# A two-block network on one core: the ends of five stages put in program order

## The chip, the core and the metric

The kernel runs on one core of a Trainium2 chip. The metric is the device time of one execution, in microseconds (us). TensorE (PE) multiplies, ScalarE (ACT) and VectorE (DVE) do elementwise work, GpSimd (POOL) takes some of it over, and SyncE (SP) issues the DMAs. Each engine runs its own instructions in the order in which the program was built, and waits on semaphores for the others.

## What is computed

The input `x` has 256 rows of 1024 columns, and six stages each add something to it:

```python
x = x + pool_mixer(rmsnorm(x))                                  # trailing means, a linear map per group
x = x + conv_ffn(rmsnorm(x))                                    # (silu(conv3(h Wg)) * (h Wv)) Wout, width 2816
x = x + chunk_attention(rmsnorm(x))                             # 16 heads, softmax, o @ w_o
x = x + conv_ffn(rmsnorm(x))
x = x + (sigmoid(ga) * y_a + sigmoid(gb) * y_b) @ w_out         # retention and stick-breaking branches
x = x + peer(rmsnorm(x))                                        # 8 heads, top-16 of 128 x 128 keys, experts u, v
```

All of it is float32.

## The kernel before

The 256 rows lie in two blocks of 128 (b = 0, 1), the 1024 columns in two halves of 512 (h = 0, 1). A float32 product is made of three matmuls on parts in a shorter type (`mm3`, lines 111 to 113): high part by high part, high by low, low by high. So every weight slab that a DMA brings (`raw`) is split: ACT writes the high part `whi` (line 73), DVE the low part `wlo` (line 81), in pieces of 512 columns; `to_pool` is the number of slabs whose low parts POOL makes instead. `prefetch(n)` sees to it that n slabs are split.

**The turn of a stage** is what stands between two stages. The stage's last products end in four accumulators `acc[b][h]`. For each, `add_to_x` (DVE, line 255) adds the accumulator to `x`, and `half_done` makes what the next stage multiplies: four transposes of 128 x 128 on PE (line 230, in `transposed`), four high parts `hT` times the norm's gain on ACT (line 236), four low parts on DVE (line 238). The squares for the norm (`sq`, line 164) are ACT's too. There are four such turns: from the first ffn to attention, from attention to the second ffn, from the second ffn to the branches, and from the branches to peer. A fifth place of the kind lies inside the branches, where the gated mix is transposed (`mT`) ahead of the last product of that stage.

**The last products before a turn.** The ffn has 22 tiles f of its inner width. `up_mm(f)` computes tile f before the gate, `act(f)` applies convolution, silu and gate on DVE and ACT and ends in the two parts `gTh` (line 216) and `gTl` (line 217), and `down(f)` multiplies them with the output weights. The products of f = 19, 20 and 21 are left for the end and written for one (b, h) after the other. In `out_proj`, which ends attention and the branches, they are those of k = 4 to 7; k is a pair of heads in attention, and the last pair is k = 7: its softmax weights `s` are scaled by DVE (line 679), transposed by PE (`pt_ps`, line 687), copied by ACT (`pT`, line 688), multiplied with the values (`o_ps`, line 722) and split into `oTh` and `oTl`.

**What sets the order.** Outside blocks marked `manual_schedule` a planner orders each engine's instructions: an instruction that is written later may go ahead of one that would wait. Inside such a block the engines named keep the order in which the program is written. The ends of the stages lie outside such blocks; `up_mm(0)` of the second ffn lies inside one for PE alone, and peer's products inside one for three engines.

Of the kernel before, what the change touches and what calls it, by code (L numbers as in the profile page):

```python
# [8 lines left out]
F32 = mybir.dt.float32  # L9
# [11 lines left out]
KT = D // 128  # L21
# [26 lines left out]
class K:  # L48
# [13 lines left out]
    def split_slab(self, later=False):  # L62
        nc = self.nc
        raw = self.loaded.pop(0)
        cols, n = raw.shape[1], self.piece
        low = nc.vector.tensor_tensor
        if self.to_pool:
            self.to_pool -= 1
            low = nc.gpsimd.tensor_tensor
        hi = self.wp.tile([128, cols], F32R, tag="hi", name="whi", bufs=self.nsplit)  # L70
        lo = self.wp.tile([128, cols], F32R, tag="lo", name="wlo", bufs=self.nsplit)
        for c in range(0, cols, n):
            i = nc.scalar.activation(hi[:, c:c + n], raw[:, c:c + n], AF.Copy)  # L73
            if self.pin:
                self.tc.keep_in_program_order(i)
                self.pin = False
# [13 lines left out]
    def start_stream(self, srcs):  # L90
# [3 lines left out]
        self.to_pool = 0  # L94
        self.pin = False

# [61 lines left out]
    def rms(self, b, out=None):  # L158
# [99 lines left out]
    def proj(self, hT, halves=2, by_block=False):  # L258
# [11 lines left out]
        if by_block:  # L270
            self.prefetch(3)
            ws = [self.next() for _ in range(halves)]
            for b in range(2):
                for half in range(halves):
                    for k in range(4):
                        part(half, k, b)
            return ps
# [25 lines left out]
    def pool_mixer(self):  # L303
        nc = self.nc
        st = self.stage
        W = WINDOWS[-1]
        order = self.tc.manual_schedule(engines={nc.tensor.engine, nc.vector.engine, nc.scalar.engine})

# [188 lines left out]
    def ffn(self, l):  # L497
# [8 lines left out]
        def up_mm(f):  # L506
# [5 lines left out]
            for k0 in range(0, KT, n):  # L512
                for i in range(2):
                    for k in range(k0, k0 + n):
                        c = slice(i * 1024 + k * 128, i * 1024 + (k + 1) * 128)
# [28 lines left out]
        if l == 0:  # L544

            with self.tc.manual_schedule(engines={nc.tensor.engine, nc.vector.engine, nc.scalar.engine}):
                up_mm(0)
# [22 lines left out]
        for f in range(2, FT, 2):  # L570
# [9 lines left out]
            if f < FT - 2:  # L580
                down(f)
        for b in range(2):
# [141 lines left out]
    def out_proj(self, rows):  # L724
# [7 lines left out]
        ws = [self.next() for _ in range(2)]  # L732
        for b in range(2):
            for h in range(2):
                for i in range(2):
                    for j in range(2):
                        self.down_part(acc, rows(4 + 2 * i + j), 4 + 2 * i + j, *ws[i], j, KT, (b,), (h,))
                self.add_to_x(acc[b][h], b, h * 512)
                self.half_done(b, h)


    def branches(self):
# [4 lines left out]
        ret = self.retention(hT, r)  # L747
        mixes = []
        for h in range(2):
            m = st.tile([128, 2, 512], F32, tag="rv", name="mix", bufs=2)  # L750
            mixes.append(m)
            for i, src in enumerate((ret, sb)):
# [9 lines left out]
        mT = []  # L762
        for h in range(2):
# [176 lines left out]
    def peer(self, rt, wq_scope):  # L940
# [3 lines left out]
        def side(gen, upto):  # L944
# [10 lines left out]
            return True  # L955

        order = ExitStack()
        order.enter_context(tc.manual_schedule(engines={nc.tensor.engine, nc.vector.engine, nc.scalar.engine}))
        with ExitStack() as ctx:
# [8 lines left out]
            prev, xn = None, []  # L968
            self.to_pool = 7
            for h in range(8):  # L970
# [14 lines left out]
                for k0 in range(0, KT, n):  # L985
                    for m in range(2):
                        for k in range(k0, k0 + n):
                            c = slice(m * 1024 + k * 128, m * 1024 + (k + 1) * 128)
# [469 lines left out]
```

## Time and profile before

| what | us |
|---|---|
| median of 3 runs | 1555.27 (1555.16 to 1555.55) |
| the profiled execution | 1555.51 |
| its span in the trace | 1553.8 |

PE is busy for 1545.5 us of the span, DVE for 1142.0, ACT for 835.3, POOL for 78.0. The span is what the trace covers; 1.7 us of the execution's time lie outside it. The chain of work that ended last runs over PE for 97% of the span.

### The profile page before, as it was taken

The numbers are of one execution on the slowest core, as the hardware profiler recorded it, in microseconds if no ns is written. First come the engines' busy times: TensorE is split into PE (matmuls) and PEld (weight loads), VectorE is DVE, ScalarE is ACT, GpSimd is POOL, SyncE is SP. The second block draws the span as 40 slices with busy tenths as digits, with TensorE's granted clock in tenths as the row PEclk, the third lists the DMA queues.
The fourth block names the chain that finished last, engine by engine and source line by source line (L and its number), as shares of the span: only waits on it lengthen the run. The fifth ranks groups of instructions, "written<-read, shape, count | busy, mean of one in ns | idle before, by whom it ended". The sixth has DMA issues, their size and how long they took to land.

```text
span 1553.8 us, 26327 instructions
## 1 busy us (share of the span) xinstructions
PE 1545.5 (99%) x10142; PEld 1383.9 (89%) x10142; DVE 1142.0 (73%) x2497; ACT 835.3 (54%) x1544; POOL 78.0 (5%) x93
## 2 busy tenths in 40 slices
PE   9999999999999999999999999999999999999999
PEld 9999987789999887888999999999999888888887
DVE  6777688876776887685689988888898655555554
ACT  7555576565555656444554555544444544454443
POOL 0000030020000202000450000000000000000000
PEclk9999999999999999999999999999999999999999
DMA  5645564335555643545426555555555656666664
GB/s 217 236 172 208 191 231 148 136 136 190 192 191 187 202 170 109 193 154 178 173 84 202 185 182 164 165 166 172 164 163 175 191 192 193 196 193 192 197 193 149
DMA packets 58157, 277.11 MB, mean 178 GB/s; under 512 B 6448, under 2 KB 7344, under 8 KB 41520
## 3 DMA queue, kind: packets, MB, share of 16 engines
q1 hardware_dynamic: 58032, 275.44, 53.5%
q8 instruction: 79, 1.29, 0.3%
q14 instruction: 46, 0.38, 0.1%
HBM read 274.36 MB, written 1.05 MB: 177 GB/s over the span
## 4 chain that ended last, share of the span: by engine, by line
PE 97%; DVE 2%; ACT 1%; DMA 0%; issue 0%; SPq 0%; POOL 0%; ACTq 0%; DVEq 0%; POOLq 0%
PE acc L112 16%; PE acc L113 16%; PE acc L111 16%; PE hps L111 8%; PE hps L112 8%; PE hps L113 8%; PE up L112 5%; PE up L113 5%; PE up L111 5%; PE gps L1066 2%; PE qps L112 1%; PE qps L111 1%; PE qps L113 1%; PE pt L230 1%; PE o_ps L722 1%; PE scps L1173 0%
## 5 line engine op out<-in xcount | busy, mean ns | idle before, releaser
L73 ACT ACTIVATE whi<-raw 128x512 fp32r<-128x512 f32 (+1 forms) x752 | 549.1, 770 | 356.7 <-PE acc L113 150.0
L81 DVE TENSOR_TENSOR wlo<-raw,whi 128x512 fp32r<-128x512 f32 (+1 forms) x568 | 447.7, 814 | 129.2 <-ACT whi L73 129.1
L111 PE MATMUL hps<-hn,whi 128*128 128x256 f32 x1024 | 291.9, 285 | 0.0
L112 PE MATMUL hps<-hn,whi 128*128 128x256 f32 x1024 | 285.8, 279 | 0.0
L113 PE MATMUL hps<-hn,wlo 128*128 128x256 f32 x1024 | 285.6, 279 | 0.0
L112 PE MATMUL up<-hT,whi 128*128 128x256 f32 x704 | 196.4, 279 | 0.8 <-DVE hT L238 0.8
L111 PE MATMUL up<-hT,whi 128*128 128x256 f32 x704 | 197.2, 280 | 0.0
L113 PE MATMUL up<-hT,wlo 128*128 128x256 f32 x704 | 196.4, 279 | 0.0
L112 PE MATMUL acc<-wlo,hn 128*128 128x512 f32 x504 | 196.1, 389 | 0.0
L113 PE MATMUL acc<-whi,hn 128*128 128x512 f32 x504 | 196.1, 389 | 0.0
L111 PE MATMUL acc<-whi,hn 128*128 128x512 f32 x504 | 196.1, 389 | 0.0
L112 PEld LDWEIGHTS hps<-hn,whi 128*128 128x128 f32 x1024 | 192.7, 188 | 0.0
L111 PEld LDWEIGHTS hps<-hn,whi 128*128 128x128 f32 x1024 | 192.6, 188 | 0.0
L113 PEld LDWEIGHTS hps<-hn,wlo 128*128 128x128 f32 x1024 | 192.4, 188 | 0.0
L88 DVE TENSOR_TENSOR wlo<-raw,whi 128x1024 fp32r<-128x1024 f32 (+1 forms) x132 | 158.7, 1203 | 14.6 <-ACT whi L73 13.7
L112 PEld LDWEIGHTS up<-hT,whi 128*128 128x128 f32 x704 | 132.4, 188 | 2.4 <-DVE hT L238 1.0
L111 PEld LDWEIGHTS up<-hT,whi 128*128 128x128 f32 x704 | 132.3, 188 | 1.5
L113 PEld LDWEIGHTS up<-hT,wlo 128*128 128x128 f32 x704 | 132.3, 188 | 0.2
L112 PE MATMUL acc<-wlo,hT 128*128 128x512 f32 x304 | 120.1, 395 | 0.0
L113 PE MATMUL acc<-whi,hT 128*128 128x512 f32 x304 | 119.8, 394 | 0.0
L111 PE MATMUL acc<-whi,hT 128*128 128x512 f32 x304 | 119.2, 393 | 0.0
L112 PEld LDWEIGHTS acc<-wlo,hn 128*128 128x128 f32 x504 | 94.6, 188 | 19.7
(290 smaller groups left out, 2395.1 us busy)
## 6 DMA issues: line engine op xcount, KB each, us to landing
raw<-in_peer_u SPq DMA_DIRECT2D x128, 512.0 KB, 3.6
raw<-in_peer_v SPq DMA_DIRECT2D x128, 512.0 KB, 3.6
raw<-in_wup SPq DMA_DIRECT2D x44, 1024.0 KB, 5.0
raw<-in_win SPq DMA_DIRECT2D x26, 1024.0 KB, 4.9
raw<-in_wdn SPq DMA_DIRECT2D x22, 1024.0 KB, 5.0
raw<-in_wqkv SPq DMA_DIRECT2D x12, 1024.0 KB, 4.9
raw<-in_wo SPq DMA_DIRECT2D x8, 1024.0 KB, 4.8
raw<-in_peer_wq SPq DMA_DIRECT2D x8, 1024.0 KB, 4.9
```

Of the source, the lines that this page charges most:

```text
L73: i = nc.scalar.activation(hi[:, c:c + n], raw[:, c:c + n], AF.Copy)
L81: low(*args, op=OP.subtract)
L88: self.nc.vector.tensor_tensor(*self.low_parts.pop(0), op=OP.subtract)
L111: mm(ps, lh, rh, start=start, stop=False, skip_group_check=True)
L112: mm(ps, lh, rl, start=False, stop=False, skip_group_check=True)
L113: mm(ps, ll, rh, start=False, stop=stop, skip_group_check=True)
L230: nc.tensor.transpose(pt[:, j, :], src[:, (k + j) * 128:(k + j + 1) * 128], self.ident)
L722: mm(o[hs, t], v[b][:, hs], w[e][:, c], start=b == 0, stop=b == 1, skip_group_check=True)
L1066: nc.tensor.matmul(ps[:, j], jh[:, j], gh[:, n, j], start=n == 0, stop=n == 1)
```

## The change

All four turns and the mix inside the branches are put in program order.

- `last_products(acc, steps)` replaces the loops at the end of `ffn` and of `out_proj`. In one block that keeps the program's order on PE, DVE and ACT, it takes one (b, h) after the other: products up to the last but one tile (`steps` yields there), then the previous half's four transposes and high parts, then the products of the last tile, then low parts and `add_to_x`.
- The last half (1, 1) gets no transposes there. `finish_turn` makes them in the next stage, after a part of its first products: in `proj(by_block)` for attention and the branches, in `up_mm(0)` of the second ffn, in peer's first head. Those first products are now in program order on the three engines too.
- In `branches`, each half of the mix is transposed right after its gate, and no longer after both.
- `to_pool` and calls of `prefetch` move, and `pin`, which kept one `whi` in place, is gone.

No engine gets more or fewer instructions. The core of the diff:

```diff
-    def half_done(self, b, h):
-        if b + h == 0:
-            self.hT = self.hT_tiles()
-
-        self.transposed(*self.hT, self.x[:, b, h * 512:(h + 1) * 512], b, 4, self.gain_next + 4 * h, k0=4 * h,
-                        bank=("o", 1) if b + h == 2 else None)
-        if b + h == 2:
-            self.to_pool = 2
-            self.pin = True
+    def half_T(self, b, h, gain):
...
+        for j in range(4):
+            nc.tensor.transpose(pt[:, j, :], src[:, j * 128:(j + 1) * 128], self.ident)
+        yield
+        for j in range(4):
+            nc.scalar.activation(self.hT[0][:, 4 * h + j, t], pt[:, j, :], AF.Copy,
+                                 scale=self.gain(gain + 4 * h + j))
+        yield
+        for j in range(4):
+            nc.vector.scalar_tensor_tensor(self.hT[1][:, 4 * h + j, t], pt[:, j, :],
...
+    def last_products(self, acc, steps):
...
+        with self.manual():
+            for b in range(2):
+                for h in range(2):
+                    p = steps(b, h)
+                    next(p)
+                    if half:
+                        next(half)
+                        next(half)
+                    for _ in p:
+                        pass
+                    if b + h == 2:
+                        next(half, None)
+                    self.add_to_x(acc[b][h], b, h * 512)
+                    if half and b + h < 2:
+                        next(half, None)
+                    half = self.half_T(b, h, self.gain_next)
+        self.last_half = half
+        self.to_pool = 2
+
+    def finish_turn(self):
+        for _ in self.last_half:
+            pass
...
+            with self.manual():
+                for b in range(2):
+                    for half in range(halves):
+                        for k in range(4):
+                            part(half, k, b)
+                        if b + half == 0:
+                            self.finish_turn()
...
-            with self.tc.manual_schedule(engines={nc.tensor.engine}):
+            self.prefetch(2)
+            with self.manual():
                 up_mm(0)
...
-        for b in range(2):
-            for h in range(2):
-                for f in range(FT - 3, FT):
-                    down(f, (b,), (h,))
-                self.add_to_x(acc[b][h], b, h * 512)
-                self.half_done(b, h)
+        def steps(b, h):
+            for f in range(FT - 3, FT):
+                down(f, (b,), (h,))
+                if f == FT - 2:
+                    yield
+
+        self.last_products(acc, steps)
...
+        def steps(b, h):
+            for k in range(4, KT):
+                self.down_part(acc, rows(k), k, *ws[k // 2 - 2], k % 2, KT, (b,), (h,))
+                if k == KT - 2:
+                    yield
...
-        for h in range(2):
             mT.append([st.tile([128, 4, S], F32R, tag=n + "T", name="mT", bufs=2) for n in "qk"])
             for b in range(2):
-                self.transposed(*mT[h], mixes[h][:, b], b, 4)
+                self.transposed(*mT[h], m[:, b], b, 4)
...
+                        if m and h + k0 == 0:
+                            self.finish_turn()
```

**PE at the end of the first ffn.** The rows are products in the order in which PE runs them: output accumulator, weights, gate tile; acc_473 to acc_476 are the four (b, h), slab 2021 holds f = 19, slab 2187 holds f = 20 and 21. Before, behind the first three products of (0, 0):

```order
L111 MATMUL acc_473<-whi_2187,gTh_285 128x512 [waits Activation_49]
L112 MATMUL acc_473<-wlo_2188,gTh_285 128x512 [waits DVE_49]
L113 MATMUL acc_473<-whi_2187,gTl_286 128x512 [waits DVE_49]
L111 MATMUL acc_474<-whi_2021,gTh_285 128x512
L112 MATMUL acc_474<-wlo_2022,gTh_285 128x512
...
L111 MATMUL acc_476<-whi_2187,gTh_285 128x512
L111 MATMUL acc_473<-whi_2187,gTh_285 128x512 [waits Activation_49]
L112 MATMUL acc_473<-wlo_2188,gTh_285 128x512
L113 MATMUL acc_473<-whi_2187,gTl_286 128x512 [waits DVE_49]
```

After, at the same place:

```order
L107 MATMUL acc_473<-whi_2187,gTh_285 128x512 [waits Activation_49]
L108 MATMUL acc_473<-wlo_2188,gTh_285 128x512 [waits DVE_49]
L109 MATMUL acc_473<-whi_2187,gTl_286 128x512 [waits DVE_49]
L107 MATMUL acc_473<-whi_2187,gTh_285 128x512 [waits Activation_49]
L108 MATMUL acc_473<-wlo_2188,gTh_285 128x512
L109 MATMUL acc_473<-whi_2187,gTl_286 128x512 [waits DVE_49]
L107 MATMUL acc_474<-whi_2021,gTh_285 128x512
L108 MATMUL acc_474<-wlo_2022,gTh_285 128x512
L109 MATMUL acc_474<-whi_2021,gTl_286 128x512
```

Before, the products of f = 19 and 20 of all four accumulators stand ahead of the first one of f = 21 (the row of acc_473 that waits on ACT behind acc_476); now the first one of f = 21 is the seventh product, and those of the other accumulators stand behind it. The end of the second ffn is changed in the same way.

**PE at the end of attention.** `pt_ps` and `o_ps` are the last pair of heads, acc_3359 and acc_3365 are (0, 0) before and after, the next number is (0, 1). Before:

```order
L111 MATMUL acc_3360<-whi_3435,oTh_2411 128x512
L112 MATMUL acc_3360<-wlo_3436,oTh_2411 128x512
L113 MATMUL acc_3360<-whi_3435,oTl_2412 128x512
L111 MATMUL acc_3361<-whi_3399,oTh_2411 128x512
L687 MATMUL pt_ps_3342<-ident_65,s_3315 128x128 [waits DVE_49,PE_49]
L687 MATMUL pt_ps_3342<-ident_65,s_3315 128x128 [waits DVE_49]
L687 MATMUL pt_ps_3342<-ident_65,s_3315 128x128
L687 MATMUL pt_ps_3347<-ident_65,s_3315 128x128 [waits DVE_49,PE_49]
L112 MATMUL acc_3361<-wlo_3400,oTh_2411 128x512
L687 MATMUL pt_ps_3347<-ident_65,s_3315 128x128 [waits DVE_49]
L687 MATMUL pt_ps_3347<-ident_65,s_3315 128x128
L722 MATMUL o_ps_3352<-pT_3341,vv_3184 64x256 [waits Activation_49]
```

After, from the last product of k = 6 of (0, 0):

```order
L109 MATMUL acc_3365<-whi_3441,oTl_2402 128x512 [waits DVE_49]
L731 MATMUL pt_ps_3348<-ident_65,s_3321 128x128 [waits DVE_49,PE_49]
L731 MATMUL pt_ps_3348<-ident_65,s_3321 128x128 [waits DVE_49]
L731 MATMUL pt_ps_3348<-ident_65,s_3321 128x128
L731 MATMUL pt_ps_3353<-ident_65,s_3321 128x128 [waits DVE_49,PE_49]
L731 MATMUL pt_ps_3353<-ident_65,s_3321 128x128 [waits DVE_49]
L731 MATMUL pt_ps_3353<-ident_65,s_3321 128x128
L766 MATMUL o_ps_3358<-pT_3347,vv_3190 64x256 [waits Activation_49] x2
L766 MATMUL o_ps_3358<-pT_3347,vv_3190 64x128 x2
L107 MATMUL acc_3365<-whi_3441,oTh_2401 128x512 [waits Activation_49]
L108 MATMUL acc_3365<-wlo_3442,oTh_2401 128x512
L109 MATMUL acc_3365<-whi_3441,oTl_2402 128x512 [waits DVE_49]
```

Before, products of (0, 1) and (1, 0) stand ahead of the last pair's transposes and among them; now nothing stands there, and the three products of k = 7 come straight behind `o_ps`.

**ACT from attention into the second ffn.** Each row is one instruction or a run of equal ones; `pt_3525` and `pt_3542` are half (1, 0), `pt_3551` and `pt_3595` half (1, 1), before and after. Before:

```order
L164 ACTIVATE sq_3642,ss_3643<-x_64 128x512
L73 ACTIVATE whi_3574<-raw_3455 128x512 x3
L164 ACTIVATE sq_3659,ss_3660<-x_64 128x512
L236 ACTIVATE hT_3472<-pt_3525,vec_69 128x128 x4
L236 ACTIVATE hT_3472<-pt_3551,vec_69 128x128 x4
L559 ACT_TABLE_LOAD
L73 ACTIVATE whi_3574<-raw_3455 128x512
L164 ACTIVATE sq_3659,ss_3660<-x_64 128x512
```

After:

```order
L187 ACTIVATE hT_3465<-pt_3516,vec_69 128x128 x4
L160 ACTIVATE sq_3668,ss_3669<-x_64 128x512
L73 ACTIVATE whi_3568<-raw_3461 128x512 x3
L187 ACTIVATE hT_3465<-pt_3542,vec_69 128x128 x4
L601 ACT_TABLE_LOAD
L73 ACTIVATE whi_3568<-raw_3461 128x512
L73 ACTIVATE whi_3685<-raw_3463 128x512
L160 ACTIVATE sq_3668,ss_3669<-x_64 128x512
L187 ACTIVATE hT_3465<-pt_3595,vec_69 128x128 x4
```

Before, the high parts of both halves of block 1 stand ahead of the table load; now those of (1, 1) stand behind the load, two `whi` and `sq`.

## Rows read from the trace of the kernel before

**Rows 1.** The page, its head and its part 1.
```profile
span 1553.8 us, 26327 instructions
...
PE 1545.5 (99%) x10142; PEld 1383.9 (89%) x10142; DVE 1142.0 (73%) x2497; ACT 835.3 (54%) x1544; POOL 78.0 (5%) x93
```

**Rows 2.** Waits of PE: line, releaser; us in total, times, longest.
```profile
PE acc L111 <- ACT mT L216: 0.3, 1, 0.3
```

**Rows 3.** Timeline (start us, duration, engine, line), PE, end of first ffn.
```profile
200.44 0.39 PE L111 MATMUL acc<-whi,gTh 128*128 128x512 f32 x1
...
203.84 0.67 PE L111 MATMUL acc<-whi,gTh 128*128 128x512 f32 x2
```

**Rows 4.** Timeline, ACT and DVE, same stretch.
```profile
199.26 0.69 DVE L523 TENSOR_TENSOR gv<-up,rb 128x512 f32<-128x512 f32 x1 [0.44 <-PE up L113]
...
203.54 0.42 ACT L216 ACTIVATE gTh<-ga 128x256 fp32r<-128x256 f32 x1 [0.49 <-DVE ga L535]
```

**Rows 5.** Timeline, PE and ACT, end of second ffn.
```profile
509.32 0.39 PE L111 MATMUL acc<-whi,gTh 128*128 128x512 f32 x1
...
512.72 0.68 PE L111 MATMUL acc<-whi,gTh 128*128 128x512 f32 x2
...
512.43 0.42 ACT L216 ACTIVATE gTh<-ga 128x256 fp32r<-128x256 f32 x1 [0.49 <-DVE ga L535]
```

**Rows 6.** Timeline, PE, end of attention.
```profile
316.10 0.40 PE L111 MATMUL acc<-whi,oTh 128*128 128x512 f32 x1
...
320.80 0.51 PE L113 MATMUL acc<-whi,oTl 128*128 128x512 f32 x1
321.23 0.86 PE L722 MATMUL o_ps<-pT,vv 128*64 128x256 f32 x6
322.03 0.50 PE L111 MATMUL acc<-whi,oTh 128*128 128x512 f32 x1
```

**Rows 7.** Timeline, DVE and ACT, same stretch.
```profile
318.26 1.01 DVE L679 TENSOR_SCALAR s<-s,rinv 128x128 f32<-128x128 f32 x4
...
319.68 0.99 ACT L688 ACTIVATE pT<-pt_ps 128x384 f32<-128x384 f32 x2 [1.67 <-PE pt_ps L687]
...
322.13 0.38 ACT L216 ACTIVATE oTh<-o_ps 128x256 fp32r<-128x256 f32 x1 [1.46 <-PE o_ps L722]
```

**Rows 8.** Timeline, PE, from attention into the second ffn.
```profile
329.32 0.60 PE L230 MATMUL pt<-ident,x 128*128 128x128 f32 x4
330.27 0.66 PE L230 MATMUL pt<-ident,x 128*128 128x128 f32 x4 [0.35 <-DVE x L255]
...
331.90 0.38 PE L112 MATMUL up<-hT,whi 128*128 128x256 f32 x1 [0.78 <-DVE hT L238]
332.13 0.28 PE L113 MATMUL up<-hT,wlo 128*128 128x256 f32 x1
```

**Rows 9.** Timeline, ACT, same stretch.
```profile
330.35 2.15 ACT L236 ACTIVATE hT<-pt,vec 128x128 fp32r<-128x128 f32 x8
332.51 1.28 ACT L559 ACT_TABLE_LOAD   x1
```

**Rows 10.** Timeline, PE and ACT, from branches into peer.
```profile
757.46 2.20 ACT L73 ACTIVATE whi<-raw 128x512 fp32r<-128x512 f32 x4
...
758.03 0.39 PE L112 MATMUL qps<-hT,whi 128*128 128x256 f32 x1 [0.21 <-DVE hT L238]
```

**Rows 11.** Timeline, DVE, inside branches.
```profile
691.42 1.29 DVE L761 TENSOR_TENSOR mix<-mix,gate 128x512 f32<-128x512 f32 x2
```

**Rows 12.** Timeline, PE, the program's start and its last product.
```profile
1.13 5.07 PE L332 MATMUL idle<-ones 128*128 128x128 f32 x22 [1.13 <-DVE ones L1321]
5.99 2.10 PE L336 MATMUL xps<-ident,x 128*128 128x128 f32 x16
...
1549.55 0.39 PE L113 MATMUL acc<-whi,hn 128*128 128x512 f32 x1
```

**Rows 13.** Busy us by stretch: PE PEld DVE ACT POOL, PEclk (granted clock), DMA.
```profile
1552.00:1553.80 1.80, 0.00 (x0) 0.00 (x0) 0.00 (x0) 0.00 (x0) 0.00 (x0) 0.67 0.13 48
```

More of the change, by code (lines that the diff above doesn't have):

```diff
@@ L72, in split_slab @@
         for c in range(0, cols, n):
[L73 to L76, printed above, removed]
+            nc.scalar.activation(hi[:, c:c + n], raw[:, c:c + n], AF.Copy)
             args = lo[:, c:c + n], raw[:, c:c + n], hi[:, c:c + n].bitcast(F32)
@@ L94, in start_stream @@
         self.to_pool = 0
-        self.pin = False
     def prefetch(self, n, later=False):
@@ L172, in rms, with manual @@
         return out
-    def half_done(self, b, h):
-        if b + h == 0:
-            self.hT = self.hT_tiles()
-        self.transposed(*self.hT, self.x[:, b, h * 512:(h + 1) * 512], b, 4, self.gain_next + 4 * h, k0=4 * h,
-                        bank=("o", 1) if b + h == 2 else None)
-        if b + h == 2:
-            self.to_pool = 2
-            self.pin = True
+    def manual(self):
+        nc = self.nc
+        return self.tc.manual_schedule(engines={nc.tensor.engine, nc.vector.engine, nc.scalar.engine})
+    def half_T(self, b, h, gain):
+        nc = self.nc
+        src, t = self.x[:, b, h * 512:(h + 1) * 512], slice(b * 128, (b + 1) * 128)
+        tag, bufs = ("o", 1) if b + h == 2 else ("w", self.nw)
+        pt = self.ps.tile([128, 4, 128], F32, tag=tag, name="pt", bufs=bufs)
+        for j in range(4):
[7 more added lines that the diff above has]
+            nc.vector.scalar_tensor_tensor(self.hT[1][:, 4 * h + j, t], pt[:, j, :],
+                                           self.gain(gain + 4 * h + j),
+                                           self.hT[0][:, 4 * h + j, t].bitcast(F32), op0=OP.mult, op1=OP.subtract)
+    def last_products(self, acc, steps):
+        self.hT = self.hT_tiles()
+        half = None
+        with self.manual():
[19 more added lines that the diff above has]
+            pass
     def factor_tiles(self):
@@ L272, in proj @@
             ws = [self.next() for _ in range(halves)]
-            for b in range(2):
-                for half in range(halves):
-                    for k in range(4):
-                        part(half, k, b)
+            with self.manual():
[5 more added lines that the diff above has]
+                            self.finish_turn()
             return ps
@@ L306, in pool_mixer @@
         W = WINDOWS[-1]
-        order = self.tc.manual_schedule(engines={nc.tensor.engine, nc.vector.engine, nc.scalar.engine})
+        order = self.manual()
         N0 = 128 + W
@@ L513, in up_mm @@
                 for i in range(2):
+                    if i and l and n < KT and k0 == 0:
+                        self.finish_turn()
                     for k in range(k0, k0 + n):
@@ L544, in ffn @@
         if l == 0:
-            with self.tc.manual_schedule(engines={nc.tensor.engine, nc.vector.engine, nc.scalar.engine}):
+            with self.manual():
                 up_mm(0)
@@ L559, in ffn @@
             self.tc.keep_in_program_order(nc.scalar.preload_act_table_set("silu_and_others"))
-            with self.tc.manual_schedule(engines={nc.tensor.engine}):
+            self.prefetch(2)
+            with self.manual():
                 up_mm(0)
@@ L581, in ffn @@
                 down(f)
-        for b in range(2):
-            for h in range(2):
-                for f in range(FT - 3, FT):
-                    down(f, (b,), (h,))
-                self.add_to_x(acc[b][h], b, h * 512)
-                self.half_done(b, h)
+        def steps(b, h):
[4 more added lines that the diff above has]
+        self.last_products(acc, steps)
     def head_norm(self, raw, r):
@@ L732, in out_proj @@
         ws = [self.next() for _ in range(2)]
-        for b in range(2):
-            for h in range(2):
[L735 to L739, printed above, removed]
+        def steps(b, h):
[3 more added lines that the diff above has]
+                    yield
+        self.last_products(acc, steps)
     def branches(self):
@@ L747, in branches @@
         ret = self.retention(hT, r)
-        mixes = []
+        mT = []
         for h in range(2):
             m = st.tile([128, 2, 512], F32, tag="rv", name="mix", bufs=2)
-            mixes.append(m)
             for i, src in enumerate((ret, sb)):
@@ L761, in branches @@
                         nc.vector.tensor_tensor(m[:, b], m[:, b], gate[:, b], op=OP.add)
-        mT = []
-        for h in range(2):
             mT.append([st.tile([128, 4, S], F32R, tag=n + "T", name="mT", bufs=2) for n in "qk"])
             for b in range(2):
-                self.transposed(*mT[h], mixes[h][:, b], b, 4)
+                self.transposed(*mT[h], m[:, b], b, 4)
         self.out_proj(lambda k: [m[:, k % 4] for m in mT[k // 4]])
@@ L955, in side @@
             return True
+        self.to_pool = 7
+        self.prefetch(2)
         order = ExitStack()
-        order.enter_context(tc.manual_schedule(engines={nc.tensor.engine, nc.vector.engine, nc.scalar.engine}))
+        order.enter_context(self.manual())
         with ExitStack() as ctx:
@@ L968, in peer @@
             prev, xn = None, []
-            self.to_pool = 7
             for h in range(8):
@@ L986, in peer @@
                     for m in range(2):
+                        if m and h + k0 == 0:
+                            self.finish_turn()
                         for k in range(k0, k0 + n):
```

## Prediction

> **What bounds the kernel now.** I read the page's head first: PE is busy for 1545.5 of 1553.8 us [rows 1], so nothing but PE's time can shorten or lengthen the run, and only some 8 us of it are waits. A change of order that leaves the number of instructions alone can win a part of these 8 us; it can lose as much as it makes PE wait. Then I read the timeline of PE at each place that the change touches, and on ACT and DVE what the products there wait for. At the ends of the two ffns PE runs from product to product without a gap: the seventh product of the tail starts at 200.44, the 22nd and 23rd stand in one row at 203.84 [rows 3], so 15 products take 3.40 us, 0.227 each. At the end of attention it is the same, with the last heads' small products in between [rows 6]. The waits that stand at the turns now are small: 0.35 and 0.78 from attention into the second ffn [rows 8], about 0.3 from the branches into peer [rows 10], 0.3 at the mix [rows 2]. This is all that the new order can save, 1.7 us.
>
> **The end of the first ffn.** The last gate tile, f = 21, is made by a chain that starts when PE has finished the last `up` product: DVE takes it up at 199.26, and ACT writes the high part `gTh` from 203.54 on for 0.42, to 203.96 [rows 4]. Before, PE has 22 products of f = 19 and 20 to run meanwhile, and the first product of f = 21, the second of the row at 203.84, starts at 203.84 + 0.23 = 204.07 [rows 3], 0.1 behind `gTh`: the cover fits to the tenth. After, six products stand ahead of it and it is the seventh. PE comes to it at 200.44 [rows 3]; no instruction of the chain is moved in ACT's and DVE's order there, so it can start at 204.07 and not before. The wait is 204.07 - 200.44 = 3.63 us. The 16 products that hid it are not lost, but they come behind it, where PE has work anyway. Everything behind the waiting product on PE, the next halves' products, their transposes and the first products of attention, moves by the same time; ACT and DVE then have more room, not less. The rest of this turn I take at 0.1: the transposes of half (1, 1) stand behind a `whi` and a `sq` now, which may cost up to 0.6, and small waits of before go, up to 0.3. Term: 3.7 (3.3 to 4.2).
>
> **The end of the second ffn.** The same: the seventh product starts at 509.32, the first one of f = 21 at 512.72 + 0.23 = 512.95, with `gTh` from 512.43 to 512.85 [rows 5]. Wait 3.63, term 3.7 (3.3 to 4.2).
>
> **The end of attention.** Before, from 316.10 to 322.03, 15 products of 512 columns run among the last heads' work, the first and the last of them in [rows 6]. After, three of them (k = 6 of (0, 0)) stand there and 12 come later: 12 x 0.23 = 2.7 us of cover are gone. What does PE wait for instead? DVE has scaled the last `s` at 318.26 + 1.01 = 319.27 [rows 7]. The last two transposes and their way to ACT take some 0.4, the second of the two copies `pT` 0.5 [rows 7], to 320.2; the six `o_ps` 0.86 [rows 6], to 321.1; `oTh` 0.38 [rows 7], to 321.5. So the products of k = 7 start at about 321.6, 0.4 earlier than PE goes on with products at 322.03. Net 2.7 - 0.4 = 2.3, between 2.0 and 2.6 for 0.3 us of hand-overs that I don't know.
>
> Then the turn itself. Half (1, 0)'s high parts stand behind a `sq` and three `whi` as before, but the half now goes to its low parts alone, and these start only when all four high parts are done; eight high parts take 2.15 [rows 9], so four take 1.1. By ACT's order I get a wait of about 0.9 for the first high part, 0.9 for the first low part, and 0.5 for (1, 1), whose parts now stand behind the table load of 1.28 [rows 9] and two `whi`. That is 2.3 against 0.35 + 0.78 in brackets, or 1.5 by the times from start to start [rows 8]. Net 0.6, between 0 and 1.0. Term: 2.3 + 0.6 = 2.9 (2.0 to 3.6).
>
> **The branches into peer.** The same pattern without a table load. Before, the first low part is waited for for 0.2 to 0.4 (the bracket leaves the drain of the product before it out) [rows 10]. After, half (1, 0) gets its high parts behind three of the four `whi` that take 2.20 [rows 10], 1.65, of which some 0.7 lie beside the last three products; with the low parts behind it I get 1.5 in all. Term: 1.1 (0.6 to 1.6).
>
> **The mix.** The second half's transposes stand as before, and the wait of 0.3 for `mT` [rows 2] goes, since the first half's parts are long there. But the first half's transposes now stand right behind its gate, and PE comes to them while DVE still adds, to 691.42 + 1.29 = 692.71 [rows 11]: about 0.4. Term: 0.1 (0 to 0.3).
>
> The moved calls of `prefetch`, `to_pool` and the lost `pin` I cost at nothing: the same slabs are loaded by SP and the same number of low parts goes to POOL at each turn, and behind PE's new waits slab work is early rather than late. If that cover fails, it is a piece of `wlo` that PE waits for, half a microsecond each time.
>
> Sum: 3.7 + 3.7 + 2.9 + 1.1 + 0.1 = 11.5 us. The profiled execution took 1555.51, 0.24 more than the median, so I add to the median: 1555.3 + 11.5 = 1566.8.
>
> **The clock.** Two stretches of before show PE at half clock. At the program's start 22 small products take 5.07 us, 230 ns each, and the 16 behind them 2.10, 131 ns each [rows 12]; the clock's column reads full there, so it is the spacing that tells it. PE had no work before 1.13, and worked some 5.1 us before the pace doubled. At the end the last product starts at 1549.55 [rows 12], and over 1552.0 to 1553.8 the granted clock is 0.67 [rows 13]: full for a third and half for two thirds, so it falls at about 1552.6, when PE has been without a product for some 2.7 us. The two new waits of 3.6 us are longer than that. Whether a wait between busy stretches brings the clock down no row shows. If it does, PE works at half pace behind the wait: 5.1 us of it, as at the start, cost 2.5 us, and no fall costs nothing. I take 1.7 for a fall, nearer to the end that a row shows, and count two falls, one at each ffn: 3.4.
>
> The Trainium skill (TensorE: Matmul & The Clock Gate, What's actually happening) says that half clock is the array's default and that only sustained activity brings the full clock back. It speaks against this change, since a long wait would be paid twice, and by it alone I would take the start's full price, 1571.8; rows 12 agree with it as far as start and end go.
>
> **The rivals.**
> - *Waits and two falls of the clock*: 1566.8 + 3.4 = 1570.2. For it: both waits are longer than the idle time ahead of the fall at the end. A third fall, in the 4 us of thin work at attention's end, would give 1571.9.
> - *Waits, no fall*: 1566.8. For it: the clock was seen to fall only where PE had no more work at all.
> - *Smaller waits, no fall*: both ffns at 3.3, attention at 2.0, peer at 0.6, which makes 9.2 and 1564.5. For it: what I put at the turns' ends comes from ACT's order, not from a row.
> - *Not slower*: PE passes over a product that waits and takes the next that is ready. Then the products of (0, 1) that are ready cover the gate tile as before, and the last heads too, and only the waits at the turns go: 1555.3 - 1.7 = 1553.6. It decides from the point at which 12 ready products, 2.7 us, can be pulled ahead. Against it: where `up` waits for `hT`'s low part until 331.90, the next product in the order needs no low part of `hT` and yet starts behind it, at 332.13 [rows 8].
> - *The change doesn't do what it says*: the built order shows the moved products where I have them, so I give this nothing of its own.
>
> **How the numbers follow.** Chances: two or three falls 0.58, waits without or with one fall 0.28, smaller waits 0.10, not slower 0.04. The likeliest gives 1570.2. The range must keep the first two cases and most of the third: from 1564.5, the third case, to 1574.5, which is the forecast with the upper ends of attention and peer (+1.2), both ffns at 4.2 (+1.0) and two falls at 2.5 (+1.6), 1574.0, and half a microsecond for a third. A measurement of this kernel can tell about 0.2%, 3.1 us, from no change: all slower cases lie 9 us or more above. Slower 0.96, same 0.03 (the last rival's 1.7 us are within 0.2%), faster 0.01.
>
> **What would show it.** Among PE's waits two new rows, the product of `acc` that waits on ACT's `gTh`, near 3.6 us each; at the end of attention waits of `pt_ps` for `s` of about 1.3 and of `o_ps` for `pT`; from attention into the second ffn and into peer waits of `up` and `qps` for `hT`, together about 2 us more than now. PE's idle time grows by some 11 us while its number of products stays. In the stretches behind the two ffn waits the granted clock reads below 1 if it falls, and products stand 450 ns apart; if it reads 1 throughout, the second case holds. The prediction would be wrong if `gTh` of f = 21 came earlier than now, or if products of (0, 1) were seen to start ahead of the one that waits.

## Result, and the profile after

The changed kernel takes 1572.13 us (median of 4 runs, 1571.99 to 1572.57) against 1555.22 before: a ratio of 1.0109, with a 95% interval of 1.0097 to 1.0121. It is slower by 16.9 us; 1570.2 was predicted, with a range of 1564.5 to 1574.5. The profiled execution has a span of 1570.9 us against 1553.8 [rows 1].

The waits of PE in the changed kernel (line, releaser; us in total, times, longest), those that answer to the four turns:

```profile
PE acc L107 <- ACT gTh L253: 6.8, 2, 3.4
PE acc L109 <- DVE rs L148: 2.0, 1, 2.0
PE pt_ps L731 <- DVE s L723: 1.1, 1, 1.1
...
PE qps L108 <- DVE hT L191: 0.8, 1, 0.8
...
PE up L108 <- DVE hT L191: 0.7, 1, 0.7
PE acc L107 <- ACT oTh L253: 0.5, 1, 0.5
...
PE qps L107 <- ACT hT L187: 0.2, 1, 0.2
PE up L107 <- ACT hT L187: 0.2, 1, 0.2
```

Before, the only ones of this kind were the 0.35 of `pt` and the 0.78 of `up` [rows 8], the 0.2 of `qps` [rows 10] and the 0.3 for `mT` [rows 2]. The first row is the forecast one: two waits of 3.4 us for `gTh`. The second, `acc` for 2.0, is in no step of the prediction.

PE at the end of the first ffn after, the place of [rows 3]:

```profile
200.43 0.39 PE L109 MATMUL acc<-whi,gTl 128*128 128x512 f32 x1
204.22 0.50 PE L107 MATMUL acc<-whi,gTh 128*128 128x512 f32 x1 [3.40 <-ACT gTh L253]
...
204.92 0.63 PE L109 MATMUL acc<-whi,gTl 128*128 128x512 f32 x1
205.35 0.63 PE L107 MATMUL acc<-whi,gTh 128*128 128x512 f32 x1
...
207.91 0.67 PE L184 MATMUL pt<-ident,x 128*128 128x128 f32 x4
208.34 0.48 PE L107 MATMUL acc<-whi,gTh 128*128 128x512 f32 x1
208.65 0.40 PE L108 MATMUL acc<-wlo,gTh 128*128 128x512 f32 x1
208.88 0.39 PE L109 MATMUL acc<-whi,gTl 128*128 128x512 f32 x1
```

The seventh product stands at 204.22 instead of right behind the sixth at 200.43, as was worked out. New is the 0.63 beside some products: from 204.92 on they stand 0.43 us apart instead of 0.23, up to the transposes at 207.91; from 208.65 on the distance is 0.23 again. The granted clock says the same, in stretches at the first ffn (three rows), at attention's end and at the second ffn (busy us of PE, PEld, DVE, ACT, POOL; then PEclk, the granted clock; DMA's share and GB/s):

```profile
200.50:204.20 3.70, 0.32 (x2) 0.00 (x0) 3.22 (x7) 2.37 (x6) 0.00 (x0) 1.00 0.40 170
204.20:207.90 3.70, 3.68 (x9) 2.75 (x10) 1.12 (x2) 0.72 (x2) 0.00 (x0) 0.56 0.85 283
207.90:210.00 2.10, 2.10 (x12) 1.82 (x11) 0.69 (x2) 1.14 (x4) 0.00 (x0) 0.97 0.00 0
325.00:328.00 3.00, 2.53 (x11) 1.19 (x10) 0.02 (x1) 1.23 (x3) 0.00 (x0) 0.58 0.65 273
...
521.50:525.20 3.70, 3.64 (x10) 2.72 (x11) 1.12 (x2) 0.73 (x3) 0.00 (x0) 0.58 0.82 283
```

Where PE works behind the two waits the clock is 0.56 and 0.58 of 2.4 GHz, most of the stretch at the lower of its two levels, and behind the first it reads 0.97 from 207.90 on, so that it is back at full some 3.8 us after PE goes on at 204.22. In the last heads' stretch at the end of attention it is 0.58 too.

How late PE is can be read at every place: both kernels run 10142 products, and away from the turns the product with the same number is the same one. The difference of the two start times, worked out from the traces:

| between | PE later by, us | predicted, without the clock | with it |
|---|---|---|---|
| start and the first ffn's end | 0.2 | 0 | 0 |
| first ffn's end to attention | 5.0 | 3.7 | 5.4 |
| attention's end into the second ffn | 3.4 | 2.9 | 2.9 |
| second ffn's end | 5.1 | 3.7 | 5.4 |
| first products of the branches | 2.3 | 0 | 0 |
| the mix | -0.2 | 0.1 | 0.1 |
| branches into peer | 1.3 | 1.1 | 1.1 |
| sum | 17.1 | 11.5 | 14.9 |

### The profile page after: what moved, and what is told of

Read it like the earlier page. It is cut to its first block, busy times and chain, and to the rows that moved or that the text cites. A ratio compares the mean times of both kernels' runs of the same rounds, so it can differ in the third digit from the quotient of the medians.

```text
span 1570.9 us, 26333 instructions
## 1 busy us (share of the span) xinstructions
PE 1551.7 (99%) x10142; PEld 1387.4 (88%) x10142; DVE 1144.3 (73%) x2497; ACT 835.6 (53%) x1544; POOL 77.0 (5%) x93
## 3 DMA queue, kind: packets, MB, share of 16 engines
q8 instruction: 79, 1.29, 0.3%
## 4 chain that ended last, share of the span: by engine, by line
PE 95%; DVE 3%; ACT 1%; DMA 1%; issue 0%; SPq 0%; POOL 0%; ACTq 0%; DVEq 0%; POOLq 0%
PE acc L108 15%; PE acc L107 15%; PE acc L109 15%; PE hps L107 8%; PE hps L108 8%; PE hps L109 8%; PE up L108 5%; PE up L109 5%; PE up L107 5%; PE gps L1111 2%; PE qps L108 1%; PE qps L109 1%; PE qps L107 1%; DVE wlo L78 1%; PE o_ps L766 1%
## 5 line engine op out<-in xcount | busy, mean ns | idle before, releaser
L107 PEld LDWEIGHTS acc<-whi,hn 128*128 128x128 f32 x504 | 94.6, 188 | 19.8
```

The lines of the kernel that those rows point to most:

```text
L107: mm(ps, lh, rh, start=start, stop=False, skip_group_check=True)
```

## The wait that nobody had on the list

The timeline of PE at the first products of the branches in the changed kernel:

```profile
540.65 0.39 PE L108 MATMUL acc<-wlo,hT 128*128 128x512 f32 x1
543.03 0.50 PE L109 MATMUL acc<-whi,hT 128*128 128x512 f32 x1 [1.99 <-DVE rs L148]
```

That of DVE in the same stretch:

```profile
535.94 5.15 DVE L904 SCALAR_TENSOR_TENSOR rtab<-rope,rg 128x128 f32<-128x128 f32 x4 [1.54 <-DMA rg<-in_ret_q_norm]
...
542.63 0.34 DVE L191 SCALAR_TENSOR_TENSOR hT<-pt,vec,hT 128x128 fp32r<-128x128 f32 x1
```

And that of POOL:

```profile
530.57 10.38 POOL L78 TENSOR_TENSOR wlo<-raw,whi 128x512 fp32r<-128x512 f32 x8 [182.51 <-ACT whi L73]
```

PE stops at 540.65 for the third product of a group, which needs the low parts of half (1, 1). DVE makes the first of them at 542.63. Ahead of it in DVE's order stand the four tables `rtab` for the rotation (retention's constants, not touched by the diff), which the planner has put there: DVE waits 1.54 us for the DMA that brings their gains and then takes 5.15 us for the four, 1.29 each. What goes on beside them is on the third fence: POOL is making low parts of weights all the while, 8 pieces from 530.57 on, 1.30 each, and DVE's instructions go in step with them, one for one.

DVE in the kernel before, two of its four tables and the low parts:

```profile
522.12 0.28 DVE L862 SCALAR_TENSOR_TENSOR rtab<-rope,rg 128x128 f32<-128x128 f32 x1
...
522.38 1.34 DVE L862 SCALAR_TENSOR_TENSOR rtab<-rope,rg 128x128 f32<-128x128 f32 x1
...
526.42 1.12 DVE L238 SCALAR_TENSOR_TENSOR hT<-pt,vec,hT 128x128 fp32r<-128x128 f32 x4
```

And POOL there:

```profile
522.27 1.30 POOL L81 TENSOR_TENSOR wlo<-raw,whi 128x512 fp32r<-128x512 f32 x1 [4.85 <-PE pt L230]
524.07 5.11 POOL L81 TENSOR_TENSOR wlo<-raw,whi 128x512 fp32r<-128x512 f32 x4 [0.50 <-ACT whi L73]
```

Two tables started ahead of POOL's piece at 522.27 and took 0.29 and 0.28; the other two started behind a piece that was still running and took 1.34 and 1.39. The low parts stood behind the tables then too, but PE did not wait for them.

## Experiments

The time before, taken beside each group of runs, was 1554.97, 1554.83 and 1555.09. The four runs of the changed kernel lie within 0.6 us; those of the kernels below spread over 0.6 to 5.6 us, and where they spread their mean granted clock does too (0.995 to 1.0). So I read single costs from the traces and use the medians for sums.

### A filler instead of the wait: is it idleness that brings the clock down?

```diff
         def steps(b, h):
             for f in range(FT - 3, FT):
+                if b + h == 0 and f == FT - 1:
+                    spare = self.ps.tile([128, 512], F32, tag="o", name="spare", bufs=1)
+                    for i in range(15):
+                        nc.tensor.matmul(spare, gT[0][:, FT - 3, 0:128], dn[(FT - 3) // 2][0][:, 1024:1536],
+                                         start=i == 0, stop=i == 14, skip_group_check=True)
                 down(f, (b,), (h,))
```

> The changed kernel with 15 useless products (the product of f = 19 again, into a bank that nobody reads) put on PE between the sixth and the seventh product at the end of each ffn. The gate tile is as late as before, so PE does useful work no earlier; but PE is no longer idle, 15 x 0.227 = 3.4 us of each wait are filled. Theory 'the clock falls because PE is idle': in the changed kernel the products behind the two waits stand 427 ns apart for 3 us, which costs some 1.5 us at each ffn; with the filler they stand 228 ns apart and the time falls by 3.0, from 1572.1 to 1569.1. Rival 'the slow pace has another cause' (fresh gate tile, first products behind a wait): 1572.1, and the 427 ns stay.

Measured: 1569.09 (1.0088, 1.0074 to 1.0102), 2.8 less than the change against the time before of the same day. PE at the first ffn's end:

```profile
199.78 0.39 PE L109 MATMUL acc<-whi,gTl 128*128 128x512 f32 x1
200.00 3.56 PE L630 MATMUL spare<-whi,gTh 128*128 128x512 f32 x15
203.57 0.50 PE L107 MATMUL acc<-whi,gTh 128*128 128x512 f32 x1
203.91 0.40 PE L108 MATMUL acc<-wlo,gTh 128*128 128x512 f32 x1
...
204.38 0.40 PE L107 MATMUL acc<-whi,gTh 128*128 128x512 f32 x1
```

Fifteen useless products fill the gap. The seventh useful one starts 3.79 us behind the sixth (199.78 to 203.57), just as in the changed kernel (200.43 to 204.22), but behind it products stand 0.23 apart. Nothing useful was moved, so the 2.8 us are the clock's, 1.4 for each ffn. The rival, that a fresh gate tile or a first product is slow by itself, falls.

### Nine products moved ahead: is the wait lost cover?

```diff
         def steps(b, h):
-            for f in range(FT - 3, FT):
-                down(f, (b,), (h,))
-                if f == FT - 2:
-                    yield
+            if b + h == 0:
+                down(FT - 3, (0,), (0,))
+                down(FT - 2, (0,), (0,))
+                down(FT - 3, (0,), (1,))
+                down(FT - 3, (1,))
+            else:
+                down(FT - 2, (b,), (h,))
+            yield
+            down(FT - 1, (b,), (h,))
```

> The changed kernel with the nine products of f = 19 of the accumulators (0, 1), (1, 0) and (1, 1) moved ahead of the first product of f = 21, in both ffns; else the program order of the change stays. Theory 'what is lost at the ffns is cover, and the clock's fall on top': 9 x 0.227 = 2.05 us of each wait of 3.6 come back, the wait that is left (1.6) is too short for the clock to fall, which gives back 1.5 more: 2 x 3.55 = 7.1, less up to 1.0 for each turn, since only three products now stand between an addition to x and the transposes that need it: 1565.0 to 1567.0. Rival 'any wait of more than a microsecond brings the clock down': 2 x 2.05 less the same, 1568.0 to 1570.0.

Measured: 1565.00 (1.0065, 1.0051 to 1.0079). The wait in its trace:

```profile
PE acc L107 <- ACT gTh L253: 3.6, 2, 1.8
```

Each wait went from 3.4 to 1.8, and no stretch behind it is at half clock in the profiled execution, which took 1563.4; the slowest, 1566.3, had a mean clock of 0.998. Whether the clock fell behind these waits there, or at attention's end, an execution without a trace doesn't tell. The wait lost 1.6 of the 2.04 us of cover that the nine products are, since `gTh` itself comes 0.4 later: by the trace ACT splits a slab ahead of it there (two `whi`, to 203.41), where in the changed kernel it waits for DVE. By PE's start times each ffn's end costs 2.6 instead of 5.0. So it was lost cover, and the forecast range was met at its lower end; whether waits of 1.8 us are safe stays open.

### The tables behind the low parts

```diff
+            late = st.tile([128, 1], F32, name=f"late{which}")
+            nc.vector.tensor_scalar(late, r[1], 0.0, (1.0, 0.125)[which], op0=OP.mult, op1=OP.add)
             for b in range(2):
-                nc.vector.scalar_tensor_tensor(t[:, b], rope[:, b], (1.0, 0.125)[which], g,
+                nc.vector.scalar_tensor_tensor(t[:, b], rope[:, b], late, g,
```

> The changed kernel with the four rope table products of the retention branch (DVE) made to depend on the norm factor of block 1, so that they stand behind the low parts of half (1, 1) on DVE and no longer ahead; two tiny instructions are added. Theory 'PE's wait of 2.0 us at the start of the branches comes from DVE's queue, where the tables (5.15 us for four, after 1.54 of waiting for a DMA) hold up the low parts': the wait goes and the time falls by 2.0 to 2.3, to 1569.9. Rival 'the low parts are late because the high parts on ACT or the transposes are': 1572.1.

Measured: 1570.99 (1.0101, 1.0085 to 1.0116), from 1567.63 to 1573.27. The median is 0.9 lower against the time before, and the spread hides whether it is 2. The trace does not: the wait of 2.0 is gone from PE's list, and PE is no later behind the first products of the branches than ahead of them. DVE and POOL at the place:

```profile
537.00 0.34 DVE L191 SCALAR_TENSOR_TENSOR hT<-pt,vec,hT 128x128 fp32r<-128x128 f32 x1
...
540.22 1.13 DVE L906 SCALAR_TENSOR_TENSOR rtab<-rope,late,rg 128x128 f32<-128x128 f32 x4
```

```profile
530.05 10.23 POOL L78 TENSOR_TENSOR wlo<-raw,whi 128x512 fp32r<-128x512 f32 x8 [183.67 <-ACT whi L73]
```

The first low part comes at 537.00, right behind the four high parts. And the four tables, which now stand where POOL has just ended (530.05 and 10.23 make 540.28), take 1.13 us instead of 5.15. Their factor comes from a tile here and not from the program, but that is not what makes them fast: the unchanged instruction took 0.28 in the kernel before where POOL was idle, and 1.34 and 1.39 beside POOL. So it is POOL that slowed them.

### The end of out_proj as before

```diff
...
-        def steps(b, h):
-            for k in range(4, KT):
-                self.down_part(acc, rows(k), k, *ws[k // 2 - 2], k % 2, KT, (b,), (h,))
-                if k == KT - 2:
-                    yield
-
-        self.last_products(acc, steps)
+        for b in range(2):
+            for h in range(2):
+                for k in range(4, KT):
+                    self.down_part(acc, rows(k), k, *ws[k // 2 - 2], k % 2, KT, (b,), (h,))
+                self.add_to_x(acc[b][h], b, h * 512)
+                self.half_done(b, h)
+        self.last_half = iter(())
```

> The changed kernel with the end of out_proj as before (planner's order, half_done), so that the turns from attention into the second ffn and from the branches into peer are undone; the two ffns keep the change. Theory 'each turn costs what the offset of PE's products shows': 3.4 us for attention and 1.4 for peer come back: 1567.3. Rival 'the new order of the next stage's first products (three engines in program order there) costs it, not out_proj': at most the 2.3 of attention's end, 1569.8, with the waits of up and qps still there.

Measured: 1567.10 (1.0078, 1.0064 to 1.0092). Its waits of PE:

```profile
PE acc L107 <- ACT gTh L262: 6.8, 2, 3.4
PE acc L109 <- DVE rs L148: 2.0, 1, 2.0
...
PE up L108 <- DVE hT L284: 0.7, 1, 0.7
...
PE pt L276 <- DVE x L301: 0.3, 1, 0.3
PE qps L108 <- DVE hT L284: 0.3, 1, 0.3
```

The waits for `s` and `oTh` at attention's end are gone, those of `up` and `qps` are nearly what they were before, and the ffns' are untouched: 4.8 us forecast, 4.8 found by the medians. The five runs lie between 1565.80 and 1570.07, so that the agreement to a tenth is luck; by PE's start times attention's end gives back 3.5 and peer 1.1, 4.6 in all. In this execution the clock also fell behind the wait of 2.0 in the branches, which it did not in the changed kernel.

### Cover for attention's end alone

```diff
...
         def steps(b, h):
-            for k in range(4, KT):
+            for k in range(4 if not ahead or b + h == 0 else 5, KT):
+                if ahead and b + h == 0 and k == KT - 1:
+                    for bh in ((0, 1), (1, 0), (1, 1)):
+                        one(4, *bh)
...
```

> The changed kernel with the nine products of k = 4 of the accumulators (0, 1), (1, 0) and (1, 1) at the end of attention moved ahead of k = 7 of (0, 0); the branches' end keeps the change. Theory 'the end of attention costs its lost cover, and the clock on top': 9 x 0.23 = 2.05 us of the 2.3 come back, and the thin stretch in which PE ran at half clock in the changed kernel's trace (products of the last heads at half pace, some 1.1 us) is filled: 3.1 in all, 1572.1 to 1569.0; the wait of pt_ps for s (1.1) goes. Rival 'cover alone': 1570.0. Rival 'the last heads' own chain sets the time': 1572.1.

Measured: 1569.92 (1.0092, 1.0077 to 1.0108), 1.8 less than the change against the time before; by the trace the place costs 0.9 instead of 3.4. Of this gain of 2.5, the wait of `pt_ps` gave up 0.9 (1.1 to 0.2), the 0.5 for `oTh` is gone, and so is the stretch at half clock; but `up`'s wait for `hT` grew from 0.7 to 1.2. With 1.1 for the clock these make 2.0; the other 0.5 stands in no wait of the list. The median is that of the rival 'cover alone' (1570.0), but the trace doesn't bear the rival out: it shows the clock's part given back as well, 2.5 for a forecast of 3.1. What hides it is the first ffn, where the half clock lasted longer in this execution and PE came out 6.3 later instead of 5.0.

### Both ends as before

The edits of 'The end of out_proj as before', and the same in the ffn:

```diff
...
-        self.last_products(acc, steps)
+        for b in range(2):
+            for h in range(2):
+                for f in range(FT - 3, FT):
+                    down(f, (b,), (h,))
+                self.add_to_x(acc[b][h], b, h * 512)
+                self.half_done(b, h)
+        self.last_half = iter(())
```

> The changed kernel with the ends of the ffns and of out_proj as before (planner's order, half_done); what stays of the change are the three engines' program order of the next stages' first products, the moved calls of prefetch and to_pool, and the mix transposed half by half. Theory 'the loss is all in the program order of the last products and their transposes': the time before, 1555.0, less 0.2 for the mix, 1554.8. Rival 'the rest costs something of its own, through POOL's low parts or the tables at the start of the branches': up to 2.3 more, 1557.3, with a wait of PE for hT's low part at the start of the branches.

Measured: 1554.79 (11 runs, 1.0000, 0.9991 to 1.0009). Everything else in the change, the moved calls of `prefetch` and `to_pool`, the program order of the next stages' first products on three engines and the mix, costs nothing in sum that can be measured. DVE's four tables take 0.28 each here, since POOL is idle when they run, and PE waits 0.3 for the low parts:

```profile
PE acc L109 <- DVE hT L284: 0.3, 1, 0.3
```

By PE's start times the first products of the branches come 0.6 later here than before, and the ends of the two ffns 0.3 earlier each: small terms of both signs stay, and what they come from was not tried.

### The ffns alone as before

The ffn's edit just shown, with `half_done`; `out_proj` keeps the change.

> The changed kernel with the ends of the two ffns alone as before; out_proj keeps the change. Theory 'the turns add up': the two ffns cost 5.0 and 7.3 us by the offset of PE's products, so 1572.1 - 12.3 = 1559.8, which is the time before plus 3.4 for attention and 1.4 for peer. Rival 'the 2.2 us at the start of the branches don't hang on the ffn's end but on the next stage's order': 1562.0, with the wait for hT's low part still there.

Measured: 1558.36 (8 runs, 1.0025, 1.0015 to 1.0036). PE at attention's end:

```profile
317.80 1.07 PE L740 MATMUL pt_ps<-ident,s 128*128 128x128 f32 x6 [1.14 <-DVE s L732]
319.05 1.26 PE L775 MATMUL o_ps<-pT,vv 128*64 128x256 f32 x8 [0.18 <-ACT pT L741]
320.79 0.50 PE L107 MATMUL acc<-whi,oTh 128*128 128x512 f32 x1 [0.47 <-ACT oTh L262]
```

The ffns' ends took 13.4 us of the 16.9 (16.9 less the 3.5 that are left), 1.1 more than forecast, and the wait at the start of the branches falls from 2.0 to 0.2 with them. Attention's end costs 2.3 by the trace here, not the 3.4 of the changed kernel: the two waits are the same (1.14 for `s`, 0.47 for `oTh`), but the transposes and `o_ps` run at full pace, 1.07 and 1.26 us, where the changed kernel needs 1.50 and 2.12. Its own rows:

```profile
323.90 1.50 PE L731 MATMUL pt_ps<-ident,s 128*128 128x128 f32 x6 [1.14 <-DVE s L723]
325.40 2.12 PE L766 MATMUL o_ps<-pT,vv 128*64 128x256 f32 x8
328.00 0.50 PE L107 MATMUL acc<-whi,oTh 128*128 128x512 f32 x1 [0.47 <-ACT oTh L253]
```

So 1.1 of the 3.4 are the clock's, in a stretch of many short waits and little work.

### Program order with the cover in it

The last products of the ffns in another order, written out by hand in the same kind of block:

```diff
...
+            for bh in ((0, 0), (0, 1), (1, 0), (1, 1)):
+                one(FT - 3, *bh)
+                if bh != (1, 1):
+                    one(FT - 2, *bh)
+            prev = None
+            for bh in ((0, 0), (0, 1), (1, 0), (1, 1)):
+                one(FT - 1, *bh)
+                self.add_to_x(acc[bh[0]][bh[1]], bh[0], bh[1] * 512)
+                if bh == (0, 1):
+                    one(FT - 2, 1, 1)
+                if prev:
+                    next(T[prev])
+                    next(T[prev])
+                    next(T[prev], None)
+                T[bh] = self.half_T(*bh, self.gain_next)
+                prev = bh
...
```

> The changed kernel with another program order at the end of the two ffns, still written out by hand and kept on the three engines: first all products of f = 19 and 20 but those of f = 20 of (1, 1), 21 in all, then f = 21 of (0, 0) and of (0, 1), f = 20 of (1, 1), the transposes of (0, 0), and so on; out_proj and the start of the branches keep the change. Theory 'it is the cover that was lost, not the planner': 15 products, 3.4 us, stand in each wait of 3.6 again and the clock stays up, so of the 5.0 us that each ffn's end costs some 0.4 are left: 1572.1 - 9.2 = 1562.9; the wait of 2.0 at the start of the branches stays. Rival 'program order on three engines costs of itself, through ACT's and DVE's order behind it': above 1566.

Measured: 1559.04 (9 runs, 1.0028, 1.0018 to 1.0038), better than expected by 3.9. Its waits of PE:

```profile
PE pt_ps L748 <- DVE s L740: 1.1, 1, 1.1
PE qps L108 <- DVE hT L191: 0.8, 1, 0.8
...
PE up L108 <- DVE hT L191: 0.7, 1, 0.7
PE acc L107 <- ACT oTh L253: 0.5, 1, 0.5
```

Both waits for `gTh` are gone, and so is the one in the branches, which was expected to stay: with the ffn's end on time POOL has ended when the last two tables run, and these take 0.28 again. The clock stays up at attention's end as well.

### All of it mended

The ffns' hand order, the tables behind the low parts, the end of `out_proj` as before.

> The kernel with the ffns' new hand order, with the rope tables behind the low parts, and with the end of out_proj as before. Theory 'the costs found are all and add up': 1562.9 less 2.2 (tables), 3.4 (attention) and 1.4 (peer): 1555.9, within 0.2% of the time before (1554.9). Rival 'a cost is still hidden': 1558 or more. A time below 1554 would mean that this order beats the planner's.

Measured: 1554.96 (11 runs, 0.9999, 0.9990 to 1.0008). What PE waits for at the turns is what it waited for before:

```profile
PE up L108 <- DVE hT L284: 0.7, 1, 0.7
...
PE pt L276 <- DVE x L301: 0.3, 1, 0.3
PE qps L108 <- DVE hT L284: 0.3, 1, 0.3
```

No cost is left over, and nothing is gained: this order and the planner's are equal. None of these kernels is measurably faster than the kernel before.

## Why the prediction was right, point by point

- **The ffns' ends** (3.7 each, and 1.7 for the clock). Right in mechanism and nearly in size: 3.56 us from start to start beyond the usual distance (200.43 to 204.22 less 0.23), and 1.4 to 1.5 for the clock. The filler takes away the clock's part, the hand order the whole; nine products ahead take away 1.6 of the 2.0 us of wait that they should.
- **The clock** (two falls, 3.4). It fell three times, for 1.5, 1.1 and 1.5, 4.1 in all. The price of 1.7 lay between the ends that I took and is a little too high for this execution; the third fall, which I had as a further case, came. [rows 12] had shown 5.1 us of half clock from rest; behind the first ffn's wait it was some 3.4 us (0.56 over 3.7 us is half clock for 0.88 of them, 0.97 over the next 2.1 for 0.06). In three traces of the experiments it lasted about twice as long at one of the two ffns, and that end cost 6.1 to 6.3 instead of 5.0: a fall has no single price.
- **Attention's end** (2.9). By the kernel with the ffns as before, 2.3 without the clock. The 2.3 that I worked out for the last pair of heads holds; the 0.6 for the turn behind it does not. It was also mis-added: the 2.3 less 1.5 that the prediction gives are 0.8. There PE waits 0.19 + 0.65 after against 0.35 + 0.78 before [rows 8]: the three `whi` ahead of the high parts ran beside products, and the parts behind the table load were early enough. I had added ACT's durations without what PE does meanwhile.
- **Peer** (1.1) and **the mix** (0.1): 1.3 and -0.2.
- **`prefetch`, `to_pool` and `pin`** (nothing). The moved calls by themselves cost nothing in sum (both ends as before, 1554.79), but the reason that I gave beside them is the step that failed: that slab work behind PE's new waits is early and so harmless, and that DVE has more room. I had counted that the same number of low parts goes to POOL, and not asked what DVE has to do beside them, and not what stands on DVE between the turn and the low parts of the half that is now finished late. The price that I named if the cover fails, half a microsecond, was wrong too: it was 2.3. It came from DVE's queue, where all four tables met POOL's pieces. The late end of the ffn is what brings them together: the ffns as before and the hand order don't have this wait of 2.0, and neither has the kernel with nine products ahead.
- The sum came out 2.2 below the trace's 17.1: 2.3 for the step that was missed, 0.7 for the clock, 0.2 at the program's start, less 0.6 for attention's turn and some tenths elsewhere. The measured time lies in the range although it holds a wait that no term stood for: its upper end had been made for attention, peer, the ffns and dearer falls. That part is luck.

The rival that PE passes over a waiting product fell with the first row of the waits: twelve ready products stood behind the seventh, and PE waited.

## What to carry to other kernels

When an order is fixed by hand, count for each operand that is made late how many instructions lie between the point at which its maker can start and its first use, on the engine that bounds the kernel: here 22 products of 0.227 us hid a chain of 5 us to the tenth, and leaving 6 of them in front cost all the rest. A wait on TensorE can cost more than its length, since the products behind it may run at half clock: 3.6 us of wait were 5.0 us of time here. And a step that moves in time moves beside other work: what another engine does in the same memory at that moment belongs into the sum.

## What the runs showed of the hardware that was not expected

- DVE's `scalar_tensor_tensor` of 128 x 128 with two inputs from SBUF takes 0.28 us with POOL idle and 1.29 us while POOL runs a `tensor_tensor` of 1.30 us; each of the four ends within 0.2 us of one of POOL's. DVE's low parts, one of whose inputs comes from PSUM, take 0.28 each beside POOL (four in 1.12 at 526.42 in the kernel before). The Trainium skill (SBUF — State Buffer, SBUF: two separate sides) says that the two engines share a pair of ports under an exclusive lock, held for a whole instruction, and that a DVE operation with two SBUF inputs needs it against a POOL operation that reads SBUF; the traces agree, 1.13 us for four instructions against 5.15.
- The granted clock fell in the middle of a kernel, at waits of 3.4 us, at all eight places in the four traces that have them: at five up to 1.5 us behind the wait, at three already during it, and at these three it stayed at the lower level about twice as long. Behind the wait of 2.0 us in the branches it fell in one of four traces (`out_proj` as before), and behind 1.8 us it did not fall in the one trace with such waits. At attention's end it fell in a stretch of short waits with small products in between in the changed kernel's trace and with the filler, and not in four others with the same waits there. So below 3.4 us the length of one wait doesn't tell by itself whether the clock falls.
